# First matrix of layer 0's feed-forward stage, computed by tokens with one of eight row pairs in seven products

## The chip, the core and the metric

The kernel runs on one core of a Trainium2 chip. The metric is the device time of one execution in microseconds; lower is better. Three runs of the kernel before the change took 2592.18, 2594.22 and 2595.54 us (median 2594.22).

The engines named below are TensorE (PE in the profile; its weight loads are a row of their own, PEld), VectorE (DVE), ScalarE (ACT), GpSimd (POOL) and SyncE (SP), whose queue issues the loads from memory.

## The reference

Two decoder layers over 256 tokens of width 2048. Layer 0 mixes tokens by retention, layer 1 by a short convolution; each is followed by a SwiGLU feed-forward stage. The part that the change touches is the feed-forward stage of layer 0:

```python
def swiglu(h, w_in, w_out):
    a, b = jnp.split(h @ w_in, 2, axis=-1)
    return (jax.nn.silu(a) * b) @ w_out
...
h = (rms_norm(x, norm2_g[i]) * (1.0 + sc2) + sh2)
x = (x + g2 * swiglu(h, ffn_w_in[i], ffn_w_out[i]))
```

`w_in` is 2048 x 11264 (5632 columns for `a`, 5632 for `b`) and `w_out` is 5632 x 2048. The scales, shifts and gates (`sc2`, `sh2`, `g2` and their like) come from the modulation, a matrix of 6 x 2048 columns per layer times one vector.

## The kernel before

**Precision and the unit of work.** Everything is float32. A float32 operand is split into a rounded high part (float32r) and the rest, and a product is the sum of three: high x high, high x low, low x high. Below, a *unit* is one 128 x 128 block of weights against all 256 tokens.

**Two ways to multiply.** *By channel* (`product`, L447 and L450): the weight block stays in the array and the activations stream past it. The high part of the weights meets both parts of the activations at once (512 columns), the low part meets the high part (256 columns): two matmuls per unit, and the result lies with channels on partitions. *By token* (`by_token`, which calls `thrice`, L460 to L462): 128 tokens of activations stay in the array and 512 weight columns stream past, three matmuls; for two token halves that is six matmuls of 512 columns for four units. The result lies with tokens on partitions and has to be turned before it can feed the next matrix.

**Sevens.** `Seven` takes two row tiles and two blocks of 512 columns (16 units) as a 2 x 2 problem in Strassen-Winograd form: seven products in the place of eight, so 7 x 3 = 21 matmuls in the place of 24. It needs sums and differences of the activations (`tokens_sums_of`), of the weights (the pieces 2 to 5 in `prepare`) and of the results (`mixed_sums`).

**Weights.** All weights lie in one array `w_all` in the order of use, in chunks of 128 x 2048 (1 MB, 16 units). `fetch` loads a chunk into one of three `raw` buffers. `prepare` makes a half of it (128 x 1024) into `hi` on ACT (L402) and `lo` on DVE (L405); a chunk of sevens takes four pieces and three more DVE operations (L391, L395, L397). `take` calls `prepare` so that `ahead_now` halves are ready beyond the one in use, 2 in most of the kernel and 3 (`AHEAD + 1`) in layer 1's feed-forward stage; there are four `hi` and four `lo` buffers.

**Modulation.** 160 of the 192 loads of `w_mod`, 1 MB each, are spread over the kernel by `paced`, which counts units: from unit 1984 to 5184 one load for each 28.8 units. Each takes one of the same three `raw` buffers and one DVE operation of 128 x 2048 (L318), whose place in DVE's order is put back (`MOD_PRIO`). A group of more than 64 units sets the allowance of `paced` to zero.

**Order.** PE's order is that of the program. The orders of the other engines are made by a scheduler from the order of the program and priorities.

**Feed-forward stage of layer 0.** It runs in two parts, each 22 of the 44 tiles of the hidden width: the first matrix (`FFN_IN`), then the second (`FFN_OUT`) by `output`. The first six columns of the first part go through `normed`, beside the norm. All others are by channel, one column tile of 16 units after the other; for each pair of them (`a` and `b`) DVE and ACT make the sums of the two halves of a bank (L504, L506), SiLU, the product (L1064, L1066) and its split (L511, L512) into `mid`.

**Feed-forward stage of layer 1.** The same shape of matrix, but by token: `last_in` puts four tiles through `first_rows` by channel and the other forty in ten *fours* (four tiles of `a`, four of `b`: 128 units). `gathered` runs the eight row pairs of a four; `IN_SEVEN = (3, 4, 6)` names the pairs in sevens. `last_input` adds the banks, applies SiLU and the product, and hands `turned` to the list `waiting`: eight transposes on PE (L1331), a copy on ACT and a subtraction on DVE. They run before the third pair of the next group (`TURNS_AT = 2`).

The lines that touch the argument most:

```python
    def thrice(o, x, w, first, last):
        (hi, lo), (w_hi, w_lo) = x, w
        nc.tensor.matmul(o, hi, w_hi, start=first, stop=False)
        nc.tensor.matmul(o, hi, w_lo, start=False, stop=False)
        nc.tensor.matmul(o, lo, w_hi, start=False, stop=last)
```

Of the kernel before, what the change touches and what calls it, by code (L numbers as in the profile page):

```python
# [17 lines left out]
P = 128  # L18
# [92 lines left out]
def halves(rows):  # L111
    n = rows // P // 2
    return [range(n), range(n, 2 * n)]


# [11 lines left out]
def ffn_in_groups():  # L127
    n = FT // 2
    cols = [[part * DFF + j * P for j in range(s * n, (s + 1) * n) for part in range(2)] for s in range(2)]
    return [led(cols[0]), [Group([c]) for c in cols[1]]]  # L130


# [5 lines left out]
FFN_IN = ffn_in_groups()  # L138
FFN_OUT = out_groups(halves(DFF), 2, LEAD_FFN)
# [27 lines left out]
def last_in():  # L167

    n, rows = LAST_TILES[0], [(i, [2 * i, 2 * i + 1]) for i in range(KT // 2)]
# [3 lines left out]
    return firsts, [[in_pairs([j * P, DFF + j * P], rows, IN_SEVEN) for j in js] for js in fours]  # L175


def last_out(part):

    first, n = part * LAST_TILES[0], LAST_TILES[part]  # L180
    order = list(range(n // 2))
    if not part:
        a, b = order[-2:]
        order = order[:5] + [a, order[6], b, order[5], order[7]]
    rows = [(i, [first + 2 * i, first + 2 * i + 1]) for i in order]
# [11 lines left out]
LAST_FIRSTS, LAST_IN = last_in()  # L197
# [3 lines left out]
def in_use_order():  # L201
# [10 lines left out]
    for layer in range(DEPTH):  # L212
# [5 lines left out]
        for part in range(2):  # L218
            ins, outs = FFN_IN[part], FFN_OUT[part]
            if layer == DEPTH - 1:  # L220
                ins, outs = sum(LAST_IN[part], [] if part else LAST_FIRSTS), sum(LAST_OUT[part], [])
            for g in ins:
                yield "ffn_w_in", layer, g
# [33 lines left out]
def trunk(ctx: ExitStack, tc: tile.TileContext, x_in, c_in, pos_in, w_mod, cols_in, gain_in, tab_in, w_all, out):  # L257
# [26 lines left out]
    at = [0]  # L284

    def taken(n):
        at[0] += n
        return cols[:, at[0] - n : at[0]]
# [4 lines left out]
    assert at[0] == n_cols  # L293
# [7 lines left out]
    differences = flat[2]  # L301
# [74 lines left out]
    def prepare(between=None):  # L376
# [13 lines left out]
        if piece == 2:  # L390
            nc.vector.tensor_tensor(differences, whole[:, DV : 3 * DV], whole[:, : 2 * DV], op=ALU.subtract)  # L391
        elif piece == 3:
            raw = differences
        elif piece == 4:
            nc.vector.tensor_tensor(b[1], b[2], differences[:, :DV], op=ALU.subtract)  # L395
# [257 lines left out]
    def output(groups, act, which, last, after=None, base=None):  # L653
# [4 lines left out]
        banks = product(first, act, base, last=False)  # L658
# [20 lines left out]
    with ExitStack() as inner:  # L679
# [372 lines left out]
        h = rows_at(0)  # L1052

    mixing = ctx.enter_context(ExitStack())
    mpool = mixing.enter_context(tc.tile_pool(name="mpool", bufs=1))
# [11 lines left out]

    for part, groups in enumerate(FFN_IN):
        mid = [mpool.tile([P, 2, S], F32R, tag=f"mid{i}", name=name("mid")) for i in range(FT // 2)]
        pending, done = [], 0  # L1070
        for i, g in enumerate(groups):
            pending += [sums(g)] if part or i else normed(acc, 0, 1, g)
            while len(pending) >= 2:
                g1, m = [tmp(tag, pool=mpool, bufs=2) for tag in ("silu", "m")]
                silu_times(*pending[:2], g1, m)
                pending = pending[2:]
                split(mid[done], m)
                done += 1
        acc = output(FFN_OUT[part], mid, (0, GT2), part == 1, (lambda j: scaled_only(1, 0, j)) if part else None)
# [33 lines left out]
    def mids(n):  # L1113

        return [mpool.tile([P, 2, 2, S], F32R, tag=f"mid{i}", name=name("mid")) for i in range(n // 2)]

    first_mid = mids(max(LAST_TILES))[: LAST_TILES[0] // 2]
    xt = [mpool.tile([P, D], F32, tag=f"xt{t}", name=f"xt{t}") for t in range(2)]

    def at(v, c):  # L1120
        return v[:, c * DV : (c + 1) * DV]
# [8 lines left out]


# [7 lines left out]
    def tokens_sums_of(a11, a21, a12, a22, third, others):  # L1139

        u = tmp("u512", (P, DV), pool=mpool, bufs=3)
        s1, s2, s4, s3 = [u[:, n * P : (n + 1) * P] for n in range(4)]
        nc.vector.tensor_tensor(s3, a11, a21, op=ALU.subtract)
        nc.vector.tensor_tensor(s1, a21, a22, op=ALU.add)
        nc.vector.tensor_tensor(s2, s1, a11, op=ALU.subtract)
        nc.vector.tensor_tensor(s4, a12, s2, op=ALU.subtract)
        split(third, s3)
        n = 3 * P // len(others)
        for i, dst in enumerate(others):
            split(dst, u[:, i * n : (i + 1) * n])  # L1150

    def parts(both):

        return [both[:, i, t * P : (t + 1) * P] for i in range(2) for t in range(2)]

    in_sums = {}

    def made_in_sums():

        tmp("beside_sums", (P, BESIDE_SUMS), bufs=1)  # L1160
        for tag, n in (("u", 3), ("low", 3), ("sum", 4)):
            single_sums.extend(tmp(tag, (P, 2, P), F32R, bufs=n) for _ in range(n))
        for i in IN_SEVEN:
            both = tmp("u512", (P, 2, S), pool=mpool, bufs=3)
            for n in range(2):
                k = 2 * i + n
                high, low = [h[k].bitcast(F32)[:, v, :] for v in range(2)]
                nc.vector.tensor_tensor(both[:, n, :], high, low, op=ALU.add)
            in_sums[i] = [single_sums.pop() for _ in range(3)]
            tokens_sums_of(*parts(both), h[2 * i][:, :, P:], in_sums[i])  # L1170

    def three(v):
        return [v[0][:, :, n * P : (n + 1) * P] for n in range(3)] if len(v) == 1 else v

# [4 lines left out]
    gain_of = []  # L1179
    gate_row = dram.tile([KT, P], F32, tag="gate_row", name="gate_row")  # L1180
# [16 lines left out]

    def flat_bank():
        return bank().rearrange("p a b -> p (a b)")
# [24 lines left out]
    def sevens(g, act, base, sums, ours, banks, first, last):  # L1224

        s1, s2, s4 = [[v[:, n, :] for n in range(2)] for v in sums]
        (a11, s3), (a12, a22) = [[half_of(act[k - base], t) for t in range(2)] for k in g.ks]
        p1, p5, p6, p7 = [(b, first, last) for b in banks]
        for use, x, (o, a, z) in zip(g.uses(), (s4, a12, s1, s3, a11, s2, a22), (
            (ours[0, 1], False, False), (ours[0, 0], False, False), p5, p7, p1, p6, (ours[1, 0], False, False)  # L1230
        )):
            thrice(o, x, take(*use), a, z)
            if use[2] in ("B21", "T3", "T2"):
                paced(4)
        paced(4)

    def mixed_sums(banks):

        p1, p5, p6, p7 = banks
        u1, u3 = at(flat[3], 0), at(flat[3], 1)  # L1240
        u2, u4 = [tmp("u512", (P, DV), pool=mpool, bufs=3) for _ in range(2)]
        nc.scalar.copy(u1, p1)
        nc.vector.tensor_tensor(u2, p6, u1, op=ALU.add)
        nc.vector.tensor_tensor(u3, p7, u2, op=ALU.add)
        nc.vector.tensor_tensor(u4, p5, u3, op=ALU.add)
        nc.vector.tensor_tensor(u2, p5, u2, op=ALU.add)
        return {(0, 0): u1, (1, 0): u3, (1, 1): u4, (0, 1): u2}

# [18 lines left out]
    waiting = []  # L1267

    def gathered(groups, act, base, sums, beside=None, mixed=None):

        ours = {(t, j): flat_bank() for t in range(2) for j in range(2)}
        banks, n = [], len(sums)
        for i, g in enumerate(groups):
            if beside:
                beside(i)
            if i == TURNS_AT and waiting:
                waiting.pop(0)()
            if isinstance(g, Seven):
                n -= 1
                banks = banks or [flat_bank() for _ in range(4)]  # L1280
                of = sums[(g.ks[0] - base) // 2]
                sevens(g, act, base, of, ours, banks, n == len(sums) - 1, n == 0)
                if not n:
                    extra = mixed_sums(banks)
                    if mixed:
                        mixed(extra)
                continue
            if len(g.cols) == 1:
                tail = TAIL_ROWS if g is groups[-1] else 0
                late, j = [], g.cols[0] // DV % 2  # L1290
                for k in g.ks:
                    weights = take(g, k, *g.items[0])
                    rows = (act[k - base], False, k == g.ks[-1])
# [145 lines left out]
```

## Time and profile before

| | us |
|---|---|
| median of three runs | 2594.22 |
| the profiled execution, own time | 2593.25 |
| its span, first to last instruction | 2591.5 |
| layer 0 feed-forward: norm and first six columns | 780.45 to 816.28 |
| rest of the first matrix, part one (608 units) | 816.28 to 1027.14 |
| second matrix, part one (352 units) | 1027.14 to 1149.16 |
| first matrix, part two (704 units) | 1149.16 to 1393.22 |
| second matrix, part two (352 units) | 1393.22 to 1515.32 |
| convolution stage of layer 1 | 1515.32 to 1873.54 |
| feed-forward stage of layer 1 | 1873.54 to the end |

The boundaries are the starts of the first matmul of each kind in the trace. How to read the views: a row of a table by stretches gives a stretch of the span, its length, then the busy time of PE, PEld, DVE, ACT and POOL with the number of instructions in brackets, the granted clock of PE, the busy share of the DMA engines and GB/s. A row of grouped instructions gives line, engine, operation, tiles, shapes, count, then busy time and the mean of one in ns, then the engine's idle time before them. A row of waits gives engine, line, what it waited for, then the total in us, the number of times and the longest. Matmuls overlap: one that lasts 390 ns lets the next start after some 230 ns, so PE's work is costed by start-to-start times, not by the mean duration.

### The profile page before, as it was taken

How to read it: one execution, taken by the hardware profiler on the slowest of the kernel's cores; microseconds unless marked ns; L12 is line 12 of the kernel's file. 1: busy time of each engine (PE TensorE's matmuls, PEld its weight loads, DVE VectorE, ACT ScalarE, POOL GpSimd, SP SyncE). 2: the span in 40 equal slices, each digit the busy share in tenths (PEclk: the TensorE clock that was granted, in tenths of full speed). 3: DMA queues.
4: the chain of work that ended last, by engine and by line, in shares of the span. 5: the costliest groups of instructions: out<-in, count | busy, mean ns of one | idle time of the engine just before them, and what ended most of it. 6: DMA issues, size and time to landing. Idle time of an engine off the chain costs nothing.

```text
span 2591.5 us, 36408 instructions
## 1 busy us (share of the span) xinstructions
PE 2563.3 (99%) x14181; PEld 2236.3 (86%) x14181; DVE 2197.4 (85%) x2762; ACT 1306.0 (50%) x1792; POOL 125.9 (5%) x232
## 2 busy tenths in 40 slices
PE   7999999999999999999999999999999999999998
PEld 6898889888889888888888898888998888888887
DVE  7988978787698887777778889988989998999978
ACT  5544543444456545334444454444565554556554
POOL 0000000110000000100001001000000000000001
PEclk9999999999999999999999999999999999999999
DMA  9975768767676888777877768877845565555654
GB/s 398 388 293 209 268 243 306 300 248 277 251 282 246 330 323 307 301 296 298 298 294 283 298 237 313 330 297 277 308 165 210 188 223 205 180 210 187 222 208 147
DMA packets 96688, 689.56 MB, mean 266 GB/s; under 512 B 10737, under 2 KB 12161, under 8 KB 13441
## 3 DMA queue, kind: packets, MB, share of 16 engines
q1 hardware_dynamic: 96514, 687.23, 71.3%
q8 instruction: 111, 1.82, 0.3%
q14 instruction: 63, 0.52, 0.1%
HBM read 685.08 MB, written 2.11 MB: 265 GB/s over the span
## 4 chain that ended last, share of the span: by engine, by line
PE 94%; DVE 3%; DMA 2%; issue 1%; ACT 1%; ACTq 0%; POOLq 0%; POOL 0%; DVEq 0%
PE bank L447 30%; PE bank L450 16%; PE bank L461 12%; PE bank L460 12%; PE bank L462 12%; PE bank L495 2%; PE bank L496 2%; PE bank L494 2%; PE bank L627 1%; PE bank L629 1%; PE bank L628 1%; DVE raw L755 1%; DMA raw<-w_all 1%; DVE lo L405 1%; PE bank L983 1%
## 5 line engine op out<-in xcount | busy, mean ns | idle before, releaser
L402 ACT CAST hi<-raw 128x1024 fp32r<-128x1024 f32 (+1 forms) x954 | 978.9, 1033 | 1015.8 <-PE bank L447 346.4
L405 DVE TENSOR_TENSOR lo<-raw,hi 128x1024 fp32r<-128x1024 f32 (+1 forms) x954 | 1133.9, 1197 | 322.6 <-ACT hi L402 317.3
L447 PE MATMUL bank<-h,hi 128*128 128x512 f32 x2016 | 699.3, 390 | 0.0
L450 PE MATMUL bank<-h,lo 128*128 128x256 f32 x2016 | 568.5, 282 | 0.0
L447 PEld LDWEIGHTS bank<-h,hi 128*128 128x128 f32 x2016 | 378.4, 188 | 79.2
L460 PE MATMUL bank<-hi,h 128*128 128x512 f32 x1032 | 405.0, 392 | 2.2 <-DVE rm L739 2.2
L461 PE MATMUL bank<-lo,h 128*128 128x512 f32 x1032 | 404.3, 392 | 0.0
L462 PE MATMUL bank<-hi,h 128*128 128x512 f32 x1032 | 402.7, 390 | 0.0
L450 PEld LDWEIGHTS bank<-h,lo 128*128 128x128 f32 x2016 | 381.0, 189 | 0.1
L318 DVE SCALAR_TENSOR_TENSOR raw<-raw,cb 128x2048 f32<-128x2048 f32 x160 | 365.5, 2284 | 15.7 <-DMA raw<-w_mod 15.3
L447 PE MATMUL bank<-mid,hi 128*128 128x512 f32 x922 | 319.8, 390 | 0.0
L450 PE MATMUL bank<-mid,lo 128*128 128x256 f32 x922 | 260.1, 282 | 0.4 <-DVE lo L405 0.4
L460 PEld LDWEIGHTS bank<-hi,h 128*128 128x128 f32 x1032 | 194.4, 188 | 40.7 <-DVE rm L739 2.8
L462 PEld LDWEIGHTS bank<-hi,h 128*128 128x128 f32 x1032 | 194.2, 188 | 40.8
L461 PEld LDWEIGHTS bank<-lo,h 128*128 128x128 f32 x1032 | 194.5, 188 | 40.4 <-DVE lo L405 3.3
L447 PEld LDWEIGHTS bank<-mid,hi 128*128 128x128 f32 x922 | 173.1, 188 | 36.2
L450 PEld LDWEIGHTS bank<-mid,lo 128*128 128x128 f32 x922 | 174.2, 189 | 0.7 <-DVE lo L405 0.7
L447 PE MATMUL bank<-rm,hi 128*128 128x512 f32 x496 | 172.5, 390 | 0.0
L496 PE MATMUL bank<-h,lo 128*128 128x256 f32 x512 | 146.4, 286 | 4.6 <-DVE lo L405 4.6
L494 PE MATMUL bank<-h,hi 128*128 128x256 f32 x512 | 146.1, 285 | 3.4 <-ACT h L783 3.4
L495 PE MATMUL bank<-h,hi 128*128 128x256 f32 x512 | 146.1, 285 | 0.7 <-DVE h L784 0.7
L450 PE MATMUL bank<-rm,lo 128*128 128x256 f32 x496 | 139.8, 282 | 0.0
(256 smaller groups left out, 3197.4 us busy)
## 6 DMA issues: line engine op xcount, KB each, us to landing
raw<-w_all SPq DMA_DIRECT2D x456, 1024.0 KB, 4.8
raw<-w_mod SPq DMA_DIRECT2D x192, 1024.0 KB, 5.2
x<-x_in SPq DMA_DIRECT2D x4, 512.0 KB, 5.3
out<-xt SPq DMA_DIRECT2D x4, 512.0 KB, 3.0
decay<-tab_in SPq DMA_DIRECT2D x8, 128.0 KB, 2.4
x<-gate_row SPq DMA_DIRECT2D x2, 512.0 KB, 4.8
last_gain<-gain_in SPq DMA_DIRECT2D x1, 1024.0 KB, 7.2
cols<-cols_in SPq DMA_DIRECT2D x1, 152.0 KB, 8.3
```

The lines of the kernel that those rows point to most:

```text
L318: nc.vector.scalar_tensor_tensor(raw, raw, 1.0, cb, op0=ALU.mult, op1=ALU.mult, accum_out=total)
L402: nc.scalar.copy(hi, raw)
L405: nc.vector.tensor_tensor(lo, raw, hi.bitcast(F32), op=ALU.subtract)
L447: nc.tensor.matmul(pt, hi, h, start=fresh and k == g.ks[0], stop=False, skip_group_check=True)
L450: nc.tensor.matmul(pt[:, 1, :], lo, h[:, 0, :], start=False, stop=last and k == g.ks[-1], skip_group_check=True)
L460: nc.tensor.matmul(o, hi, w_hi, start=first, stop=False)
L461: nc.tensor.matmul(o, hi, w_lo, start=False, stop=False)
L462: nc.tensor.matmul(o, lo, w_hi, start=False, stop=last)
L494: nc.tensor.matmul(pt, hi, h[:, 0, :], start=first, stop=False, skip_group_check=True)
L495: nc.tensor.matmul(pt, hi, h[:, 1, :], start=False, stop=False, skip_group_check=True)
L496: nc.tensor.matmul(pt, lo, h[:, 0, :], start=False, stop=last, skip_group_check=True)
L627: nc.tensor.matmul(pt, hi, high, start=k == 0, stop=False, skip_group_check=True)
```

## The change

The first matrix of layer 0's feed-forward stage now runs as layer 1's does, with other settings:

- Parts of 20 and 24 tiles (`FFN_TILES`) replace 22 and 22. Four tiles (eight columns) run by channel through `first_rows`; the other forty run in ten fours by token through `gathered` and `ffn_input` (the old `last_input`).
- `FIRST_SEVEN = (5,)`: in each four, pair 5 of the eight is in sevens; the other seven pairs are plain. `sums_of_rows` makes the sums of activations for that pair once.
- The product of a four is turned by `turned`: before the third pair of the next four, or, after the last four of a part, inside the first group of the second matrix, before its seventh row (`TURN_ROW = 6`). `output` gets the argument `before` for it.
- `LEAD_FFN` goes from 2 to 4: the first group of the second matrix holds four columns. The rows of part one go in the order of `pair_order(0)`.
- `ahead_now` is 3 during the fours.
- The stage has its own pool `ffn`, with `differences` (layer 1 keeps it in the memory of `x`), `halves` for two of the mixed sums, `rows` for the sums, and three buffers `u512`. The activations lie at the offset `EARLIER`, and the convolution stage's pool opens after.

The core of the diff (layer 1 keeps its settings; the functions that moved are otherwise as they were):

```diff
-IN_SEVEN, OUT_SEVEN, TURNS_AT, BESIDE_CB, BESIDE_SUMS = (3, 4, 6), ((2, 4, 6), (2, 4, 6)), 2, 40, 48
-LAST_TILES = 20, 24
+FIRST_SEVEN, IN_SEVEN, OUT_SEVEN, TURNS_AT, BESIDE_CB, BESIDE_SUMS = (5,), (3, 4, 6), ((2, 4, 6), (2, 4, 6)), 2, 40, 48
+FFN_TILES = 20, 24
-LEAD_RET, LEAD_CONV, LEAD_FFN = 6, 4, 2
+LEAD_RET, LEAD_CONV, LEAD_FFN, TURN_ROW = 6, 4, 4, 6
...
-FFN_IN = ffn_in_groups()
-FFN_OUT = out_groups(halves(DFF), 2, LEAD_FFN)
...
+FFN_FIRSTS, FFN_IN = ffn_in(FIRST_SEVEN)
+_, LAST_IN = ffn_in(IN_SEVEN)
+FFN_OUT = out_groups([[k for _, r in pair_order(part) for k in r] for part in range(2)], 2, LEAD_FFN)
...
-    def output(groups, act, which, last, after=None, base=None):
+    def output(groups, act, which, last, after=None, base=None, before=None):
...
-        banks = product(first, act, base, last=False)
+        banks = product(first, act, base, before=before, last=False)
...
-    for part, groups in enumerate(FFN_IN):
-        mid = [mpool.tile([P, 2, S], F32R, tag=f"mid{i}", name=name("mid")) for i in range(FT // 2)]
-        pending, done = [], 0
-        for i, g in enumerate(groups):
-            pending += [sums(g)] if part or i else normed(acc, 0, 1, g)
-            while len(pending) >= 2:
-                g1, m = [tmp(tag, pool=mpool, bufs=2) for tag in ("silu", "m")]
-                silu_times(*pending[:2], g1, m)
-                pending = pending[2:]
-                split(mid[done], m)
-                done += 1
-        acc = output(FFN_OUT[part], mid, (0, GT2), part == 1, (lambda j: scaled_only(1, 0, j)) if part else None)
...
+    with tc.tile_pool(name="ffn", bufs=1) as mpool:
+        first_mid = mids(max(FFN_TILES))[: FFN_TILES[0] // 2]
+        own = [mpool.tile([P, 2, DV], F32, tag=tag, name=tag) for tag in ("differences", "halves")]
+        differences[:] = [own[0].rearrange("p a b -> p (a b)")]
+        halves_of = [own[1][:, n, :] for n in range(2)]
+        places = [[mpool.tile([P, 2, 3 * P], F32R, tag=f"rows{i}", name="rows")] for i in range(len(FIRST_SEVEN))]
+        for part in range(2):
+            n = FFN_TILES[part] // 2
+            mid = mids(FFN_TILES[part]) if part else first_mid
+            if not part:
+                first_rows(0, mid[-2:])
+                in_sums = sums_of_rows(FIRST_SEVEN, places)
+            ahead_now[0] = AHEAD + 1
+            for i, groups in enumerate(FFN_IN[part]):
+                ffn_input(groups, mid[2 * i : 2 * i + 2], in_sums)
+            ahead_now[0] = AHEAD
+            turn_at = FFN_OUT[part][0].ks[TURN_ROW]
+            act = [mid[k // 2][:, k % 2] for k in range(2 * n)]
+            acc = output(
+                FFN_OUT[part], act, (0, GT2), part == 1, (lambda j: scaled_only(1, 0, j)) if part else None,
+                base=part * FFN_TILES[0], before=lambda k: k == turn_at and waiting.pop(0)(),
+            )
+    h = rows_at(0)
```

The functions that layer 0 now calls, as the changed kernel has them:

```python
    def ffn_input(groups, pairs, in_sums, seven=(None, None)):
        ours, extra = gathered(groups, h, 0, in_sums)
        for (t, j), pt in ours.items():
            nc.vector.tensor_tensor(extra[t, j], pt, extra[t, j], op=ALU.add)
        ms = []
        for t in range(2):
            m = extra[t, 0]
            nc.scalar.activation(m, m, AF.Silu)
            nc.vector.tensor_tensor(m, m, extra[t, 1], op=ALU.mult)
            ms.append(m)

        def turned():
            for n, (dst, of) in enumerate(zip(pairs, seven)):
                pt = bank()
                for i in range(2):
                    for t, m in enumerate(ms):
                        c = slice((2 * n + i) * P, (2 * n + i + 1) * P)
                        nc.tensor.transpose(pt[:, i, t * P : (t + 1) * P], m[:, c], ident)
...
                nc.scalar.copy(dst[:, :, 0, :], pt)
                nc.vector.tensor_tensor(dst[:, :, 1, :], pt, dst[:, :, 0, :].bitcast(F32), op=ALU.subtract)
...
        waiting.append(turned)
```

More of the change, by code (lines that the diff above doesn't have):

```diff
@@ L174, in last_in, with pair_order @@
     fours = [[*range(0, n - 4, 4)], [*range(n, FT, 4)]]
[L175 to L181, printed above, removed]
+    return firsts, [[in_pairs([j * P, DFF + j * P], rows, sevens) for j in js] for js in fours]
+def pair_order(part):
+    order = list(range(FFN_TILES[part] // 2))
     if not part:
@@ L184, in last_out @@
         order = order[:5] + [a, order[6], b, order[5], order[7]]
-    rows = [(i, [first + 2 * i, first + 2 * i + 1]) for i in order]
+    return [(i, [part * FFN_TILES[0] + 2 * i + n for n in range(2)]) for i in order]
+def last_out(part):
+    rows = pair_order(part)
     out = []
@@ new lines, in flat_bank, with sevens @@
+    def flat_bank():
+        return bank().rearrange("p a b -> p (a b)")
+    def sevens(g, act, base, sums, ours, banks, first, last):
+        s1, s2, s4 = [[v[:, n, :] for n in range(2)] for v in sums]
+        (a11, s3), (a12, a22) = [[half_of(act[k - base], t) for t in range(2)] for k in g.ks]
+        p1, p5, p6, p7 = [(b, first, last) for b in banks]
+        for use, x, (o, a, z) in zip(g.uses(), (s4, a12, s1, s3, a11, s2, a22), (
+            (ours[0, 1], False, False), (ours[0, 0], False, False), p5, p7, p1, p6, (ours[1, 0], False, False)
+        )):
+            thrice(o, x, take(*use), a, z)
+            if use[2] in ("B21", "T3", "T2"):
+                paced(4)
+        paced(4)
@@ L1070, in trunk, with first_rows @@
+    def first_rows(layer, pairs, turns=()):
         pending, done = [], 0
-        for i, g in enumerate(groups):
-            pending += [sums(g)] if part or i else normed(acc, 0, 1, g)
+        for i, g in enumerate(FFN_FIRSTS):
+            pending += [sums(g)] if i else normed(acc, layer, 1, g)
             while len(pending) >= 2:
-                g1, m = [tmp(tag, pool=mpool, bufs=2) for tag in ("silu", "m")]
+                both = tmp("u512", (P, 2, S), pool=mpool, bufs=3)
+                g1, m = both[:, 0, :], both[:, 1, :]
@@ new lines, in last_rows, with single @@
+    def last_rows(act, base):
+        def single(g, ours, last):
+            tail = TAIL_ROWS if last else 0
+            late, j = [], g.cols[0] // DV % 2
+            for k in g.ks:
+                weights = take(g, k, *g.items[0])
+                rows = (act[k - base], False, k == g.ks[-1])
+                if tail:
+                    late.append((*weights, *rows))
+                else:
+                    by_token([ours[t, j] for t in range(2)], *weights, *rows)
+                paced(g.n)
+            for t in range(2):
+                for args in late:
+                    by_token([ours[t, j] for t in range(2)], *args, halves=[t])
+                added(t, g.cols[0] // DV, ours[t, j], True)
+                if tail:
+                    stored(t)
+        return single
```

283 lines of the change are left out of this document (123 added, 160 removed).

## The prediction

> **What bounds the kernel now.** I read the page first: its busy times, then the chain of work that ended last.
>
> ```profile
> span 2591.5 us, 36408 instructions
> ...
> PE 2563.3 (99%) x14181; PEld 2236.3 (86%) x14181; DVE 2197.4 (85%) x2762; ACT 1306.0 (50%) x1792; POOL 125.9 (5%) x232
> ...
> PE 94%; DVE 3%; DMA 2%; issue 1%; ACT 1%; ACTq 0%; POOLq 0%; POOL 0%; DVEq 0%
> ```
>
> PE holds 94% of the chain. Next the stage itself, in the table by stretches: norm with the first six columns, first matrix, second matrix, first matrix, second matrix.
>
> ```profile
> 780.45:816.28 35.83, 35.83 (x302) 35.83 (x301) 30.79 (x52) 22.30 (x38) 1.75 (x2) 1.00 0.62 228
> 816.28:1027.14 210.86, 210.86 (x1219) 186.84 (x1218) 175.60 (x212) 106.56 (x167) 16.03 (x37) 1.00 0.84 314
> 1027.14:1149.16 122.02, 122.02 (x706) 108.17 (x705) 95.37 (x105) 47.38 (x48) 11.12 (x17) 1.00 0.80 302
> 1149.16:1393.22 244.06, 244.06 (x1411) 216.37 (x1410) 190.86 (x225) 118.02 (x174) 14.14 (x25) 1.00 0.79 293
> 1393.22:1515.32 122.10, 122.10 (x729) 109.12 (x728) 102.79 (x131) 57.97 (x77) 11.69 (x24) 1.00 0.79 292
> ```
>
> PE's busy time equals the length in every row, at the full granted clock. So nothing that DVE, ACT or the loads save in this stage can shorten it; only less PE work can, and new waits can lengthen it.
>
> **The matmuls, from by channel to by token.** The stretch of part two is 704 units, so a unit costs 244.06 / 704 = 346.7 ns; part one gives 210.86 / 608 = 346.8. The change moves 1280 units, 443.8 us. The six columns beside the norm and two more columns stay by channel.
>
> The price of a four by token stands in layer 1, which runs the same fours with three sevens. From one set of transposes to the next:
>
> ```profile
> 2252.65:2295.26 42.61, 42.61 (x193) 35.09 (x191) 38.66 (x44) 24.09 (x27) 0.00 (x0) 1.00 0.55 198
> 2295.26:2337.83 42.57, 42.57 (x193) 35.10 (x192) 39.96 (x50) 25.30 (x30) 0.00 (x0) 1.00 0.55 198
> ```
>
> ```profile
> 2252.81 0.87 PE bank L1331 x8
> ...
> 2295.42 0.87 PE bank L1331 x8
> ```
>
> The code gives 5 x 24 + 3 x 21 = 183 matmuls and 8 transposes, which agrees with the 191 weight loads of the first row. The transposes hold 0.87 us of the chain, so a matmul of 512 columns costs (42.61 - 0.87) / 183 = 228.1 ns start to start. One seven in place of three means 189 matmuls: 42.61 + 6 x 0.2281 = 43.98 us for a four, 439.8 us for ten. **Gain: 443.8 - 439.8 = 4.0 us.** It has two parts. By token alone is a loss: 192 x 0.2281 + 0.87 = 44.67 us against 128 x 0.3467 = 44.38, so 2.9 us for ten fours. The seven saves 3 x 0.2281 = 0.68 in each, 6.8 us for ten.
>
> **The transposes**, 80 of them, are in that price at 0.87 / 8 = 109 ns. Their mean duration is longer:
>
> ```profile
> L1331 PE MATMUL bank<-tab,x 128*128 128x128 f32 x80 | 10.3, 272 | 0.0
> ```
>
> They overlap as the matmuls do, and 10.3 us busy over 80 is 129 ns, so I take 109 and keep 272 as the other bound: 80 x (0.272 - 0.109) = 13.0 us more. The Trainium skill ("TensorE: Matmul & The Clock Gate", Part 4: PE-mode transpose) gives some 275 ns for a transpose in a kernel's context and says that this mode does not count as busy for the clock gate. By that figure the 80 would take 22 us and the change would lose; the trace agrees on the duration, but not on its being the cost, and the granted clock is 1.00 in both rows of layer 1 that hold transposes.
>
> **DVE.** Its work per four grows. These rows are from four fours of layer 1, and the last from part two of layer 0's first matrix:
>
> ```profile
> L405 DVE TENSOR_TENSOR lo<-raw,hi 128x1024 fp32r<-128x1024 f32 x64 | 77.4, 1220 | 10.3 <-ACT hi L402 9.6
> ...
> L405 DVE TENSOR_TENSOR lo<-x,hi 128x1024 fp32r<-128x1024 f32 x12 | 14.6, 1220 | 0.7 <-ACT hi L402 0.7
> L391 DVE TENSOR_TENSOR x<-raw 128x1024 f32<-128x1024 f32 x12 | 14.6, 1217 | 0.0
> ...
> L395 DVE TENSOR_TENSOR raw<-raw,x 128x512 f32<-128x512 f32 x13 | 8.9, 683 | 0.0
> L397 DVE TENSOR_TENSOR raw<-raw 128x512 f32<-128x512 f32 x12 | 8.3, 692 | 0.4
> L405 DVE TENSOR_TENSOR lo<-raw,hi 128x512 fp32r<-128x512 f32 x12 | 8.2, 686 | 0.5 <-ACT hi L402 0.5
> ```
>
> ```profile
> L318 DVE SCALAR_TENSOR_TENSOR raw<-raw,cb 128x2048 f32<-128x2048 f32 x25 | 57.1, 2284 | 0.0
> ```
>
> A chunk of sevens costs 3 x 1.22 + 0.69 + 1.22 + 0.68 + 0.69 = 6.94 us of DVE, a plain one 2.44. Layer 1's four takes 38.66 us (the 39.96 of the other row hold sums for its second matrix, which layer 0 has not). Two sevens fewer: 38.66 - 2 x 4.50 = 29.7. The modulation, 25 in 704 units, adds 4.5 x 2.28 = 10.4. Sum 40.1 of 43.98 us, 91%; before, it is 190.86 / 244.06 = 78%. Two kinds of rows say that this can be hidden: layer 1's fours at 38.66 / 42.61 and 39.96 / 42.57 (91% and 94%), without modulation, and the convolution stage, with it:
>
> ```profile
> 1551.00:1596.00 45.00, 45.00 (x261) 39.91 (x261) 42.01 (x69) 23.68 (x41) 5.52 (x9) 1.00 0.77 285
> 1596.00:1640.00 44.00, 44.00 (x255) 39.02 (x254) 40.09 (x53) 19.41 (x27) 2.42 (x6) 1.00 0.87 332
> 1640.00:1685.00 45.00, 45.00 (x261) 39.89 (x261) 41.43 (x56) 20.39 (x29) 2.42 (x6) 1.00 0.89 333
> ```
>
> DVE is at 91 to 93% there with PE never idle. I cost DVE at nothing; what hides it are the halves ready ahead. No row has sevens and modulation together, so the bound above is the first rival's. Below nothing is excluded: PE has no idle time to give back.
>
> **Loads.** Their number stays 456 and 192, and SP issues them in the order of use. Three buffers must serve 8 + 4.5 loads per four, one per 3.5 us (3.6 before).
>
> ```profile
> raw<-w_all SPq DMA_DIRECT2D x456, 1024.0 KB, 4.8
> raw<-w_mod SPq DMA_DIRECT2D x192, 1024.0 KB, 5.2
> ```
>
> The waits in part two of layer 0's first matrix, and in the convolution stage:
>
> ```profile
> ACT hi L402 <- PE bank L447: 94.0, 68, 1.7
> ...
> ACT hi L402 <- DMA raw<-w_all: 16.8, 9, 2.7
> ```
>
> ```profile
> ACT hi L402 <- DMA raw<-w_all: 31.8, 15, 3.5
> ```
>
> ACT waits 68 times for PE to free a buffer and 9 times for a load: preparation is mostly early, sometimes up to 2.7 or 3.5 us late, and PE never felt it with two halves ahead (5.5 us of PE work). With three ahead there are 8.2 us. Cost: nothing; without that cover a late load costs PE its lateness.
>
> **The passages into the second matrix** are new: the last four of a part is turned before the seventh row of the first group, 6 x 4 units x 0.3467 = 8.3 us after the four's end. In layer 1 the four that ends 48 matmuls before the transposes at 2337.99, at about 2327, has its results ready here:
>
> ```profile
> 2327.74 0.68 DVE L1317 TENSOR_TENSOR x<-bank,x 128x512 f32<-128x512 f32 x1
> ...
> 2331.87 0.68 DVE L1322 TENSOR_TENSOR x<-x,u 128x512 f32<-128x512 f32 x1
> ```
>
> That is 5.6 us, so 2.7 are to spare, and one multiply of 2.28 fits. If it is late, PE waits with all that is queued behind the transposes, and weights ready ahead are no help. Layer 1's passage into its second matrix lost 105.50 - 104.96 = 0.54 us:
>
> ```profile
> 2094.00:2199.50 105.50, 104.96 (x467) 86.64 (x466) 90.56 (x106) 55.24 (x62) 0.00 (x0) 1.00 0.58 211
> ```
>
> I take 0.5 for each of two passages, **1.0 us**; bounds 0 and 2 x 2.3, a second multiply in the way.
>
> **What costs nothing.** The sums for the seven (some 3 us of DVE) are due 5 pairs or 27 us later. The second matrix has the same 704 units; its first group of 72 and 88 units (40 before) sets the allowance of the modulation to zero, so 2 to 3 loads come later, under DVE's 95.37 of 122.02 us. The activations' new offset is that of layer 1. The new pool's memory is taken 36 us after the last reader's end.
>
> **Sum.** -4.0 + 1.0 = -3.0 us. The profiled execution took 2593.25 (span 2591.5 and 1.75 around it), 1.0 under the median of 2594.22. From the median: **2591.2 us**.
>
> **The rivals.**
>
> *DVE is late behind the seven: slower.* The pieces of a seven take PE 6 x 0.228 = 1.37 us each instead of 2.74. A half right behind it can be started when PE frees the buffer three halves back, now only 2 x 1.37 + 0.68 = 3.4 us before its use, and needs ACT's 1.05 and DVE's 1.22. So 1.1 us of delay is free. One multiply of 2.28 in front of it costs 1.2, a late load (3.5) costs up to 2.4. At 1.5 us in each of ten fours the time is 2591.2 + 15 = 2606. For it: DVE at 91% with operations of 2.28 us between. Against it: layer 1 has two sevens in a row and lost nothing, and the multiply's place is put back behind the weights. It decides from 0.8 us per four: ten of those, 8.2 us, less the 3.0 gained, pass 0.2% (5.2 us).
>
> *The same in one four of four,* as the multiply falls by chance (4.5 in 44 us): 10 x 0.25 x 1.2 = 3 us, and the gain is gone: 2594.2, no change.
>
> *The transposes cost their duration,* 272 ns each: 2591.2 + 13 = 2604, slower. For it only the mean of that row; against it the period of 42.61 us, in which eight of them hold 0.87. It is the rule of the Trainium skill weighed above.
>
> **How the numbers follow.** Forecast 0.69, with a range of its own from 2588.5 (all of the 4.0 and 1.7 us of spread between runs) to 2593; DVE late 0.17; chance falls 0.12; transposes 0.02. What a measurement can tell from no change is about 0.2%, 5.2 us. Faster than 2589.0 needs more than the whole gain of 4.0 plus scatter: 0.15, taken from the forecast's share. Slower than 2599.4: 0.19. Between: 0.66. The range runs from 2588.5 to 2606: below it lie some 0.08, above it half of the first rival.
>
> **What would show it.** Ten periods of 44.0 us between sets of eight transposes, the last of each part followed by the second matrix, with PE idle under 0.1 us inside. DVE at about 91% there. Wrong: periods over 44.4; weight loads of PE waiting for L405 after pair 5, or ACT for loads longer than 4 us; a gap ahead of the transposes in the second matrix.

## The result

The changed kernel is slower: 2604.13 us as the median of 14 runs (2597.85 to 2611.08) against 2592.22 for the kernel before (14 runs, 2590.72 to 2595.54); the ratio is 1.0045, interval 1.0035 to 1.0055. The forecast was 2591.2, a small gain. The time lies inside the stated range (2588.5 to 2606), but on the other side of the time before, and its scatter of 13 us against 5 before is a result too: it suggests that something in the kernel now depends on chance, such as how long each load happens to take.

The profiled execution took 2599.81 us (span 2598.0), one of the three fastest of the 14, so the trace shows a part of the loss: 6.6 us between the profiled executions, 11.9 between the medians. From its page, the busy times and the chain of work that ended last:

```profile
span 2598.0 us, 35123 instructions
...
PE 2561.2 (99%) x13593; PEld 2204.8 (85%) x13593; DVE 2256.4 (87%) x2780; ACT 1295.3 (50%) x1704; POOL 132.3 (5%) x232
...
PE 88%; DVE 5%; DMA 4%; issue 1%; ACT 1%; ACTq 0%; POOLq 0%; POOL 0%; DVEq 0%
```

PE's share of the chain fell from 94% to 88%; DVE and the loads took it over. The table by stretches, from the first matmul of the stage to the first of the convolution stage, before (first fence) and after:

```profile
780.45:1515.32 734.87, 734.87 (x4356) 656.34 (x4356) 595.41 (x722) 352.22 (x503) 54.74 (x105) 1.00 0.80 297
```

```profile
778.70:1521.67 742.97, 734.60 (x3768) 625.00 (x3767) 651.89 (x736) 340.31 (x414) 58.92 (x103) 1.00 0.78 293
```

The stage is 8.1 us longer, and PE, never idle before, is idle for 8.4. The same table from one set of transposes to the next, two fours of part one and two of part two, and under it the modulation's multiply alone (each counts two instructions, the second reads its sum):

```profile
882.59:928.98 46.39, 44.75 (x198) 36.08 (x197) 40.85 (x44) 20.34 (x23) 3.89 (x6) 1.00 0.79 299
928.98:975.39 46.41, 45.07 (x199) 36.02 (x198) 43.51 (x46) 20.83 (x24) 9.04 (x10) 1.00 0.83 317
1176.84:1220.70 43.86, 43.86 (x198) 36.30 (x197) 39.73 (x42) 20.22 (x23) 3.51 (x4) 1.00 0.76 286
1265.21:1309.33 44.12, 44.12 (x199) 36.22 (x197) 40.34 (x42) 20.68 (x23) 2.59 (x4) 1.00 0.79 297
```

```profile
928.98:975.39 46.41, 13.79 (x12) 1.00 0.83 317
1176.84:1220.70 43.86, 9.71 (x9) 1.00 0.76 286
```

In part two a four takes about what the forecast said (43.98): 43.9 to 44.5 us, and PE's idle time there is one gap of 0.3 us in the four that is not shown. In part one it takes 46.4, and there up to six multiplies fall into a four in place of four or five. That is arrears: `normed` counts 96 units in one call, more than 64, so the allowance of the modulation stands at zero there; afterwards `paced` may give 0.045 x 128 = 5.8 loads per four until the plan's 4.4 is caught up.

What PE waits for is seen in the chain of waits of the first stall:

```profile
837.83 1.24 DVE lo L398
839.07 0.02 issue
839.08 7.37 DMA raw<-w_all
846.45 0.02 issue
846.48 1.23 DVE differences L384
...
851.34 1.74 DVE raw L311
...
853.57 4.91 DMA raw<-w_all
...
858.56 1.05 ACT hi L395
859.61 0.02 issue
859.64 1.24 DVE lo L398
860.87 0.04 issue
860.91 0.50 PE bank L454
```

This is a loop through one resource, the raw buffers. A `lo` is finished, 0.02 us later the load that wanted its buffer is issued, it lands 7.4 us later and is used at once; a multiply (L311) ends, and the next load is issued at once. The waits of ACT from 816 to 1020 us say the same:

```profile
ACT hi L395 <- DMA raw<-w_all: 71.6, 30, 6.4
...
ACT hi L395 <- PE bank L455: 11.5, 11, 1.7
```

Before, in part one's rest of the first matrix (816.28 to 1027.14 us):

```profile
ACT hi L402 <- DMA raw<-w_all: 39.1, 19, 4.8
...
ACT hi L402 <- PE bank L447: 25.3, 21, 1.7
```

So preparation already stood behind a load about as often as behind PE in part one, without an idle PE; now it is mostly behind a load, and later. (The 68 waits for PE and 9 for a load that the prediction went by are of part two.) Such waits alone do not show the loss: the seventh run below has 26 of them, 81.0 us, in the same window, and PE idle for 0.5 us.

### The profile page after: what moved, and what is told of

Its sections match the earlier page's. It is cut to its first block, busy times and chain, and to the rows that moved or that the text cites. A ratio compares the mean times of both kernels' runs of the same rounds, so it can differ in the third digit from the quotient of the medians.

```text
span 2598.0 us, 35123 instructions
## 1 busy us (share of the span) xinstructions
PE 2561.2 (99%) x13593; PEld 2204.8 (85%) x13593; DVE 2256.4 (87%) x2780; ACT 1295.3 (50%) x1704; POOL 132.3 (5%) x232
## 4 chain that ended last, share of the span: by engine, by line
PE 88%; DVE 5%; DMA 4%; issue 1%; ACT 1%; ACTq 0%; POOLq 0%; POOL 0%; DVEq 0%
PE bank L440 18%; PE bank L454 16%; PE bank L455 16%; PE bank L453 16%; PE bank L443 10%; DMA raw<-w_all 4%; DVE lo L398 2%; PE bank L488 2%; PE bank L489 2%; PE bank L487 2%; PE bank L620 1%; PE bank L622 1%; PE bank L621 1%; DVE raw L748 1%; DVE raw L311 1%
## 5 line engine op out<-in xcount | busy, mean ns | idle before, releaser
L453 PE MATMUL bank<-hi,h 128*128 128x512 f32 x1632 | 639.5, 392 | 4.2 <-ACT hi L395 2.1
L454 PE MATMUL bank<-lo,h 128*128 128x512 f32 x1632 | 638.9, 391 | 4.0 <-DVE lo L398 4.0
L455 PE MATMUL bank<-hi,h 128*128 128x512 f32 x1632 | 636.2, 390 | 0.0
L311 DVE SCALAR_TENSOR_TENSOR raw<-raw,cb 128x2048 f32<-128x2048 f32 x160 | 365.9, 2287 | 15.7 <-DMA raw<-w_mod 14.9
L454 PEld LDWEIGHTS bank<-lo,h 128*128 128x128 f32 x1632 | 307.0, 188 | 72.0 <-DVE lo L398 12.0
L453 PEld LDWEIGHTS bank<-hi,h 128*128 128x128 f32 x1632 | 307.1, 188 | 67.3 <-ACT hi L395 3.5
L455 PEld LDWEIGHTS bank<-hi,h 128*128 128x128 f32 x1632 | 306.6, 188 | 64.0
L440 PE MATMUL bank<-h,hi 128*128 128x512 f32 x736 | 255.4, 390 | 0.0
L443 PE MATMUL bank<-h,lo 128*128 128x256 f32 x736 | 207.4, 282 | 0.0
L440 PEld LDWEIGHTS bank<-h,hi 128*128 128x128 f32 x736 | 138.1, 188 | 28.9
L489 PE MATMUL bank<-h,lo 128*128 128x256 f32 x512 | 146.7, 286 | 4.2 <-DVE lo L398 4.2
L443 PEld LDWEIGHTS bank<-h,lo 128*128 128x128 f32 x736 | 139.2, 189 | 0.0
```

The lines of the kernel that those rows point to most:

```text
L311: nc.vector.scalar_tensor_tensor(raw, raw, 1.0, cb, op0=ALU.mult, op1=ALU.mult, accum_out=total)
L440: nc.tensor.matmul(pt, hi, h, start=fresh and k == g.ks[0], stop=False, skip_group_check=True)
L443: nc.tensor.matmul(pt[:, 1, :], lo, h[:, 0, :], start=False, stop=last and k == g.ks[-1], skip_group_check=True)
L489: nc.tensor.matmul(pt, lo, h[:, 0, :], start=False, stop=last, skip_group_check=True)
```

## The experiments

The theories. **A:** the turn-over of the three raw buffers: with six loads of the modulation and a seven in a four, a buffer comes back too late. **B:** DVE's own work. **C:** the halves right behind the seven are late because a multiply stands in front of them, the prediction's first rival. All times are medians, and each ratio is to runs of the kernel before made beside that run. The fifth run was made twice, the second and the sixth four times, the others five to fourteen times. "Idle" is PE's idle time in the stage in the one profiled execution, a sum over the gaps between its matmuls; the profiled executions of runs 3 and 7 were the fastest of theirs.

| run | us | ratio to before (95%) | idle, us |
|---|---|---|---|
| the change | 2604.13 | 1.0045 (1.0035 to 1.0055) | 8.4 |
| 1 own buffer for the modulation | 2591.52 | 0.9999 (0.9990 to 1.0008) | 3.4 |
| 2 the same, from GpSimd's queue | 2709.80 | 1.0451 (1.0435 to 1.0466) | 72.9 |
| 3 even rate | 2591.46 | 0.9999 (0.9989 to 1.0008) | 0.5 |
| 4 by token alone | 2592.33 | 1.0000 (0.9990 to 1.0009) | 0.0 |
| 5 arrears kept up | 2622.74 | 1.0118 (1.0100 to 1.0137) | 21.1 |
| 6 multiply not put back | 2606.27 | 1.0055 (1.0042 to 1.0069) | 8.8 |
| 7 filler for the seven | 2596.36 | 1.0019 (1.0009 to 1.0030) | 0.5 |
| 8 even rate and own buffer | 2591.26 | 0.9995 (0.9986 to 1.0004) | 2.3 |
| 9 ring of four | 2588.32 | 0.9984 (0.9975 to 0.9993) | 0.8 |
| 10 ring of four, even rate | 2587.63 | 0.9980 (0.9971 to 0.9988) | 0.4 |
| 11 rate 0.030 | 2614.10 | 1.0076 (1.0064 to 1.0088) | 0.7 |
| 12 ring of four, rate 0.030 | 2610.60 | 1.0067 (1.0054 to 1.0079) | 2.9 |

**1 and 2. A buffer of its own for the modulation.**

```diff
-        raw = mod_raw(t)
+        raw = mod_raw(t, *mod_place[0])
...
+        mod_place[0] = (mpool, 1)
```

> The modulation's loads of layer 0's feed-forward stage get a buffer of their own (one, in the stage's pool), so that the three raw buffers serve weights alone; SP still issues all loads in one order, so a load of the modulation that waits for its buffer holds back the weights behind it. Theory A (the turn-over of the three raw buffers, shared with 6 modulation loads per four in part one, is what PE waits for): PE's idle time in the stage falls from 8.4 us to under 3, the sets of transposes of part one come every 44.0 to 44.6 us, time 2590 to 2594. Theory B (DVE's own work is too much or comes late, whatever the buffers): DVE has the same work, the periods stay at 46, time 2598 to 2606.

> As the run before, but the modulation's loads of the stage are issued from GpSimd's queue, so that a wait for their buffer holds back no weights. Theory A: idle time under 1 us, periods of 44.0 us in both parts, time 2589 to 2592. Theory B: periods stay at 46, 2598 to 2606.

The first gives 2591.52, a time that theory A had: DVE does the same work, the rate and the seven are the same, and the loss against before is gone, though not all of the wait (3.4 us idle where A said under 3). The waits of ACT turn round (816 to 1020 us):

```profile
ACT hi L396 <- PE bank L456: 80.7, 57, 1.7
...
ACT hi L396 <- DMA raw<-w_all: 3.2, 1, 3.2
```

The second missed both expectations, 2709.8, and does not bear on A or B: it made a wait of its own. This row of its page, with the idle time of DVE at the end, was 15.7 us before the change:

```profile
L314 DVE SCALAR_TENSOR_TENSOR raw<-raw,cb 128x2048 f32<-128x2048 f32 x160 | 365.9, 2287 | 164.0 <-DMA raw<-w_mod 163.7
```

DVE stands still at the multiply until its load lands, with the weights' `lo` behind it in order. In the trace, ten of these loads between 880 and 980 us are issued 1.1 to 2.3 us after the multiply that frees their buffer ends; in the first run, from SP's queue, it is 0.03 us. Whether that delay is all of it stays open.

**3, 5, 11 and 12. The rate of the modulation.**

```diff
-        allowed[0] = min(allowed[0] + n * MOST, 2.0) if n <= 64 else 0.0
+        allowed[0] = min(allowed[0] + n * most[0], 2.0) if n <= 64 else 0.0
...
             ahead_now[0] = AHEAD + 1
+            most[0] = 0.036
```

> In the fours of layer 0 the allowance of the modulation is 0.036 loads per unit in place of 0.045, so that no four makes up arrears: 4.6 loads at most per four in place of 6 in part one. Everything else as changed. Theory A and theory B both expect that arrears were what overfilled part one (DVE 29.7 + 6 x 2.36 = 43.9 us of a four of 43.98; 14 loads through three buffers): periods of part one fall from 46.4 to 44.0 to 44.4 as in part two, time 2590 to 2594. Theory C (the halves right behind the seven are late at any rate of modulation): periods stay over 45, time over 2598.

> The plan of the modulation is made steeper over layer 0's feed-forward stage (102 loads in units 1984 to 4160 in place of 76, the convolution stage gets the fewer), so that all ten fours, not only those of part one, take up to 5.8 loads. If 6 loads per four beside a seven are too many for three buffers (theory A, and B's DVE sum of 43 us), part two's periods rise from 43.9 to 44.5 to over 45, as part one's 46.4, and the time is over 2606. If part one is slow for another reason (its start, the first rows), part two stays at 44 and the time at 2598 to 2606.

For the fifth the plan alone was changed: `(1984, 49), (4160, 151), (5184, n_mod)` in place of `(1984, 49), (5184, n_mod)`. Both came out as the arrears would have it: 2591.46 without them, 2622.74 with them in all ten fours, where part two now looks like part one or worse:

```profile
1180.05:1226.97 46.92, 44.97 (x198) 36.07 (x197) 43.44 (x46) 20.69 (x24) 2.97 (x6) 1.00 0.84 315
1226.97:1274.33 47.36, 44.48 (x198) 36.15 (x197) 44.06 (x46) 20.61 (x24) 2.79 (x5) 1.00 0.83 308
1274.33:1324.40 50.07, 46.03 (x198) 37.36 (x197) 43.42 (x46) 20.92 (x23) 2.44 (x6) 0.97 0.77 290
```

So theory C in its strict form, late at any rate, is out, and so is the thought that part one is slow because it comes first. A and B are not told apart by these two, since arrears bring multiplies as well as loads. The 0.5 us of idle time in the third run is that of its fastest execution, 2587.57; the median is 3.8 us over the tenth run's below, so its typical execution may well still wait.

> Three buffers as changed, 0.030 loads per unit in the fours (3.8 per four; the second matrix, at 0.045, makes up for them). Theory A: buffer time per four falls by one to two turns of 10 us against 4.6 loads, the periods are 43.9 and the median 2588 to 2590, lower than the 2591.5 of 0.036. If the second matrix or the convolution stage now waits for its loads, the gain comes back there: 2590 to 2596.

> The ring of four with 0.030 loads per unit in the fours: the largest reserve of all. Median 2587 to 2589 if the reserve of buffers decides; no better than the ring of four alone if that has already removed the wait.

Both missed, 2614.10 and 2610.60, though the periods of their fours are 43.9 us (the twelfth has one gap of 2.9 us, in its first four). What was put off came due before layer 1's feed-forward norm. The waits of the eleventh run there (1860 to 1900 us), one of 18.1 us:

```profile
ACT hi L395 <- DMA raw<-w_all: 25.0, 3, 21.4
PEld bank L620 <- ACT hi L395: 18.3, 1, 18.3
PE bank L620 <- ACT hi L395: 18.1, 1, 18.1
```

**4 and 7. Without the seven, and with filler in its place.** The fourth run sets `FIRST_SEVEN = ()`, and without mixed sums the banks go straight to SiLU and the product:

```diff
-            m = extra[t, 0]
-            nc.scalar.activation(m, m, AF.Silu)
-            nc.vector.tensor_tensor(m, m, extra[t, 1], op=ALU.mult)
+            m = halves_of[t]
+            nc.scalar.activation(m, ours[t, 0], AF.Silu)
+            nc.vector.tensor_tensor(m, m, ours[t, 1], op=ALU.mult)
```

The seventh adds DVE additions of 128 x 1024 from `cb` into `differences` in pairs 5 and 7 of each four, which nothing reads.

> No pair in sevens: all eight by token, the banks go straight to SiLU and the product. DVE loses 4.5 + 5.4 us per four. The sum of PE's work is 44.67 us per four: without waits 2592.2 + 2.9 = 2595 us (or 2595 to 2597 with the two passages). If the seven is needed for the delay (theories B and C), idle time is under 1 us and the time is 2594 to 2597. If the loads alone make it (theory A in its strictest form: 14 loads per four are too many for three buffers, seven or not), idle time stays over 4 us and the time is over 2599.

> By token alone as in the fourth run, with about seven DVE additions of 128 x 1024 per four that nothing needs (8 us), so that DVE is as busy as with the seven (about 42 of 44.4 us) while no chunk is held for a seven's four pieces; the output stays right. Theory B (DVE's load is enough to make the delay): idle time over 4 us in part one, time over 2598. Theory A with the seven's long hold of a buffer as the decisive part: idle time under 1.5 us, 2592 to 2595.

Two fours of part one of the fourth run, then of the seventh:

```profile
880.62:925.05 44.43, 44.43 (x201) 36.87 (x200) 33.38 (x31) 18.39 (x20) 1.87 (x5) 1.00 0.86 325
925.05:969.49 44.44, 44.44 (x202) 36.87 (x201) 35.48 (x33) 19.67 (x21) 4.20 (x10) 1.00 0.90 340
```

```profile
880.46:924.90 44.44, 44.44 (x202) 36.88 (x201) 44.41 (x42) 18.42 (x20) 4.82 (x6) 1.00 0.89 333
924.90:969.33 44.43, 44.43 (x201) 36.87 (x200) 44.34 (x42) 19.00 (x21) 10.60 (x10) 1.00 0.87 330
```

By token alone PE never waits in the stage, with the same arrears: a four costs 44.43 us against 44.38 by channel, and the kernel's time is that of before, 2592.33; the 2594 to 2597 expected was too high, by the price of a four (44.67). So loads and arrears alone do not do it. Nor is it the rate of memory, as a mean over a four: 325 to 340 GB/s here, 299 to 317 in the changed kernel's part one. With the filler DVE is busy for the whole of a four, 44.41 of 44.44 us, and PE still does not wait in the two shown. That is one execution, though, and the fastest of eight: the median, 2596.36, lies between what A (to 2595) and B (from 2598) expected and 4.0 us over the fourth run's. So DVE's load may take part, in executions that no trace shows, but the change cost far more: its 2604.1 is 15.8 us over the 2588.3 of the ninth run below, which does the same work without the wait. What the filler lacks is the seven's chunk.

How long a buffer is held can be read from the trace by pairing each load with the instructions that read its buffer, in the programmed order. Means in us over the fours of part one (landed to first read; first read to last; W a plain chunk, S a chunk of a seven, M the modulation). S is a mean over three or four chunks, and the others move by some tenths with the window chosen:

```
                        W wait, held    S wait, held    M wait, held
before (part one)       0.38  4.62      -               1.22  2.28
the change              0.29  4.16      0.04  8.04      1.98  2.29
4 by token alone        0.43  4.46      -               0.89  2.29
6 multiply not put back 0.72  4.32      0.02 10.71      0.97  2.28
7 filler                0.16  4.53      -               1.47  2.28
9 ring of four          2.90  5.22      0.78 10.14      3.17  2.28
```

The seven's chunk holds its buffer for 8 us in place of 4, since its fourth piece needs `raw` too; and the multiply waits 2.0 us in place of 0.9 to 1.2 (1.5 with the filler). Loads take 5.3 to 5.9 us on average (W and M) in all of them. In the ninth run, with a fourth buffer, chunks and multiplies wait and hold longer still, and PE does not wait: it is the number of buffers that makes a long hold cost time.

**6. The multiply not put back.** `MOD_PRIO` is 0 in the fours.

> As changed, but in the fours the modulation's multiply keeps its place in DVE's order (no priority behind the weights), so that it gives its buffer back sooner: the wait from its load's landing to the multiply, 2.0 us on average in part one, should fall under 1. Theory A: a quarter to a half of the 8.4 us of idle time goes, 2594 to 2600. Theory C (weights behind the seven are late because something stands in front of them): more multiplies stand in front of weights, idle time rises over 10 us, 2606 or more.

The multiply's wait did fall, to 0.97 us, but the seven's chunk is then held for 10.7 us, and the time stayed: 2606.27. A's partial gain did not come. C's time (2606 or more) is just met and its idle time (over 10 us) not: 8.8 us against 8.4, and the ratios, 1.0055 and 1.0045, have intervals that overlap. So this run does not settle C by itself. Reordering DVE moves the hold from one buffer to another.

**8, 9 and 10. Cures together.** The ninth run puts a fourth buffer into the shared ring:

```diff
+    def raw_place():
+        if not fourth[0]:
+            return wpool, RAW_BUFS
+        turn_of_four[0] += 1
+        return (wpool, RAW_BUFS) if turn_of_four[0] % 4 else (fourth[0], 1)
...
-        raw = wpool.tile([P, CHUNK], F32, tag="raw", name=name("raw"), bufs=RAW_BUFS)
+        pool, bufs = raw_place()
+        raw = pool.tile([P, CHUNK], F32, tag="raw", name=name("raw"), bufs=bufs)
...
+        fourth[0] = mpool
```

> The first and the third run together: a buffer of its own for the modulation and no arrears made up in the fours. If both cures act on the same wait, no period is over 44.0 us, PE's idle time in the stage is under 0.5 us, and the whole gain of PE's work shows: 43.87 us in place of 44.38 for ten fours, 5 us, less the passages: 2587 to 2589 as a median, with less scatter than either cure alone. If scatter comes from elsewhere the median stays at 2591.

> As changed, with a fourth raw buffer in the stage's own pool that takes every fourth load, weights or modulation, in the same order: DVE's work, the rate of 6 loads per four and the seven stay. Theory A (turn-over of the buffers): PE's idle time in the stage falls from 8.4 us to under 1, periods 43.9 to 44.2 in both parts, median 2588 to 2592. Theory B (DVE's load, with whatever buffers): idle time stays over 4 us, median over 2598.

> The ring of four and the even rate (0.036 in the fours) together. If the wait of the stage is then gone altogether, all periods are 43.9, the median is 2587 to 2589 and the scatter as small as before the change; if the median stays at 2591, what is left of the scatter is not this stage's.

The eighth missed by some 2 us (2591.26): its modulation has one buffer only, and four of its fours still have a gap of 0.4 to 1.0 us. The ninth decides between A and B: same DVE work, same order of loads, same multiplies, one buffer more, and 2604.13 becomes 2588.32. Two fours of its part one:

```profile
881.67:925.54 43.87, 43.87 (x198) 36.30 (x197) 42.14 (x44) 20.64 (x23) 5.19 (x6) 1.00 0.86 331
925.54:969.43 43.89, 43.89 (x198) 36.23 (x197) 42.75 (x46) 21.24 (x24) 8.00 (x9) 1.00 0.88 333
```

DVE is at 96 and 97%, and PE is without a gap while the memory gives 331 to 333 GB/s. The tenth is the best version: 2587.63, ratio 0.9980, faster than both kernels, with a scatter of 4.5 us (2585.61 to 2590.15). Its stage takes

```profile
780.63:1511.40 730.77, 730.38 (x3767) 625.86 (x3767) 637.09 (x727) 344.53 (x415) 85.80 (x95) 1.00 0.79 291
```

4.1 us less than before.

## Why the prediction was wrong

*PE's work: right.* A four was put at 43.98 us, measured 43.87; the gain of the stage at 4.0, measured 734.87 - 730.77 = 4.1 in the tenth run, with 0.4 us of waiting left. By token alone was put at 44.67 and is 44.43: it loses 0.05 per four and not 0.29, and the seven saves 0.56 per four in place of 0.68.

*The transposes: right.* They were put at 0.87 us for eight, and a set in the changed kernel's chain holds

```profile
882.75 0.88 PE bank L1177 x8
```

So that rival is out, and with it the sum by a transpose's own duration.

*DVE: the rate was mis-sized.* The sum of 40.1 us took 4.5 multiplies per four from the row of part two, where it holds (39.73 and 40.34). Part one had up to six, 40.9 and 43.5 us. The zero allowance was noted in the prediction for the second matrix and costed there; for the 96 units of `normed`, right ahead of the fours, it was not. The trace before the change had the higher rate in part one's 608 units, which is 5.5 per four:

```profile
L318 DVE SCALAR_TENSOR_TENSOR raw<-raw,cb 128x2048 f32<-128x2048 f32 x26 | 59.4, 2283 | 2.3 <-DMA raw<-w_mod 2.1
```

This alone cost PE next to nothing: the ninth run has the same work, and PE is idle for 0.8 us in its stage.

*Loads: the step that failed.* "Cost: nothing", because the number of loads per us stayed and lateness was covered by halves ahead. It cost 2.5 us (46.4 against 43.87) in each of the two fours of part one shown above, and 11.7 us over the stage of the profiled execution against the ninth run's (742.97 and 731.25), which has one buffer more and the same work. The step counted how often a buffer is needed and not how long it is held. The seven's chunk holds one twice as long, DVE's added work delays the multiply and so holds another, and the arrears ask for the third. Lateness then does not come singly, to be absorbed by 8.2 us of reserve; it is handed on from load to load around the ring, as the chain of the first stall shows. The evidence for "mostly early" was of part two, too: in part one, ACT stood behind a load 19 times in 40.

*The rows taken as proof of cover* were of other mixtures: layer 1's fours have sevens without modulation, the convolution stage modulation without sevens. The prediction said that no row has both, and still priced the mixture at nothing.

*The passages:* 1.0 us was put there; in the fourth and ninth runs PE has no gap between the end of a part's last four and its transposes. The changed kernel lost 1.6 us in the passage of part one, but to a late `lo`, not to the transposes.

*The first rival* named the right sign and nearly the time (2606), by luck: its price of 1.5 us in each of ten fours was, in the profiled execution, 2.5 in two fours of part one and 0 to 0.6 in part two. Its main reason, a multiply in front of the halves behind the seven, is not the cause: the sixth run moved the multiplies without a change clear of noise, and the ninth left them where they were and cured it. The late load that it names beside the multiply is nearer, but it was priced as one load late by itself.

Left open: where the typical run loses the 4 us that the profiled one does not (2604.13 against 2599.81). The scatter shrinks with the fourth buffer, from 13 us to 4, which points at the same ring, but no trace shows one of the slower executions. Which of the three holds matters most was not separated further: without the seven or with a fourth buffer the wait is all but gone, and without the arrears it is in the one execution that was traced.

## What to carry to other kernels

Where loads share a ring of buffers, cost an edit by buffer time: loads per stretch times (load time + wait for the reader + time until the last read), against the number of buffers times the length of the stretch. An edit that lengthens a hold, or delays the reader of another load in the ring, has a price even if the engines' sums fit and every load's rate is as before. With the table's means, 5.6 us for a load, and 5.8 loads of the modulation per four (5.5 before the change), the sum for a four of part one is an estimated 141 us in the changed kernel against 3 x 43.9 = 132, and 135 against 133 in the fourth run and before the change. By this estimate the three buffers were full already before the change, without a wait of PE. The rule was drawn from these runs; none of them tested it as a forecast. And look at rates by stretch: work spread by a plan has arrears after each group that the plan skips, and a mean over the stage hides them.

## What the runs showed of the hardware

PE's granted clock dropped after a long gap. Behind the 18 us of the eleventh run the first row stands at 0.50 and the next is back at 0.99:

```profile
1892.30:1898.00 5.70, 5.24 (x23) 4.94 (x24) 4.58 (x4) 2.78 (x3) 0.00 (x0) 0.50 0.93 336
1898.00:1910.00 12.00, 12.00 (x101) 12.00 (x101) 10.62 (x20) 7.92 (x13) 0.00 (x0) 0.99 0.51 199
```

The Trainium skill ("TensorE: Matmul & The Clock Gate", Part 1: The HAM clock gate) says that the clock is halved after an idle window of some 3.4 us and released after one of work; these rows agree, though the half clock lasted at least 5.7 us here. In the fifth run a gap of 3.3 us was enough for a short drop, which is the 0.97 of its third row above:

```profile
1300.00:1305.00 5.00, 4.24 (x11) 3.10 (x12) 4.86 (x5) 2.77 (x3) 0.00 (x0) 0.66 0.94 357
```

In the changed kernel no gap of the stage is over 1.6 us, and the clock stays at 1.00 in the fours, so its loss there is waiting alone.

DVE can be busy for all of 44.4 us, as in the two fours shown with the filler, and PE lose nothing there: the share of an engine off the chain says little until one knows what its lateness holds up.
